# Attention in three scheduler streams, y stores on SyncE, issue times in the scheduler, and first gates during the last attention round

## The chip, the cores and the metric

The kernel runs on all 8 cores of one Trainium2 chip, one batch element of 4096 x 1024 tokens per core, with the same instructions on each. The metric is the device time of the slowest core in microseconds (us). Some executions of these kernels fall in a second, slower state, in which the four cores of one die show a lower TensorE clock (0.81 instead of 0.98 in the worst); only fast runs are compared here. Single cores of a fast run differ by some 30 us. Profiles are of the slowest core unless said.

## The reference, cut to what matters

One decoder layer. From the same input come the projections of 12 attention heads (three dilated causal windows) and of a state-space mixer; then per token

```python
z = h @ w_in                      # q | k | v | u | gates
y_attn = softmax-weighted sum over the three dilated windows
y_ssm  = glu(gelu(s5_ssm(u)))
mix = (sig(g1 + b) * (y_ssm @ w_ssm_proj) + sig(g2 + b) * (y_attn @ w_attn_proj)) @ w_out
h = LN(alpha * h + mix)
h = LN(alpha * h + relu(h @ w_up)**2 @ w_down)
```

The kernel does it in two stages. The mixed stage (the first 620 us) runs projections, attention in six rounds, and the state space of 32 groups side by side. The dense stage works off eight blocks of 512 tokens: GLU, gates, output projection, layer norm, and the large MLP. TensorE bounds it.

## The kernel before

The program notes every operation with a stream name and a priority, and a list scheduler then fixes the order of each engine's queue. Within a stream the order of an engine's operations is the program's; between streams the scheduler may choose. It has a cost for each operation and a rough model of the DMA queues.

```python
if op.dma:
    issue = 1000.0 if e == "pool" else 70.0     # ns that an issue takes of the engine
    free[e] = t + issue
    start = end = max(dma_free[e][0], t + issue)
    ...
```

State space, one of 32 groups: the result leaves PSUM through ScalarE, and ScalarE also issues its two stores.

```python
def ssm_y(g):
    ...
    cp("act", ysg.ap, bk.ap.rearrange("p (t c) -> p t c", t=2), [bk], [ysg])
    for t in range(2):
        dma("act", y_d[g, :, t * 8:t * 8 + 8].rearrange("h t c -> t h c"), ysg.ap[:, t, :], [ysg], [y_res.res[g * 2 + t]])
```

Attention is a single stream, "att". In the last rounds (g = 2) every bank is evicted and normalised:

```python
for (q, j) in units:
    qk(q, j)                 # scores, TensorE
    pt = ex(q, j)            # exp on ScalarE, times bias on VectorE
    if prev is not None:
        pv(*prev)            # products; after each 4th block: evac() and norm()
    prev = (q, j, pt)
```

Weights of the dense stage are float32 in memory. GpSimd's DMA queue casts most of them to bfloat16 scratch while attention runs, one cast after every third projection tile; w_up is cast in the first dense block itself.

```python
for name in ("glu", "gate", "sp", "ap", "out", "dn"):
    for i in range(len(wb[name][2].res) // 2):
        add_cast(name, i)

def pace(op, rnd, t):
    nonlocal evs
    evs += 1
    if rnd > 0 and evs % 3 == 0 and wcast:
        after = Res(); after.w = op
        wcast.pop(0)([after])
```

The softmax here doesn't subtract the row's maximum and nothing guards it: scores larger than these inputs give would overflow.

## Time and profile before

| | kernel before |
|---|---|
| median of fast runs | 2025.7 us (2023.1 to 2030.0) |
| TensorE busy | 1863.0 us, 92% |
| last scan of the state space | 571.0 us |
| last projection tile evicted | 546.7 us |
| first transposes of the dense stage | 688.4 us |
| TensorE's wait for w_up | 14.6 us |

The transposes of the first layer norm make a good clock: they come after exactly 271 matmuls of the dense stage, so their time says how far the work has come. The table by stretch, cut at such marks (columns: stretch, length, then busy us and instruction count of each engine, TensorE clock, DMA share, GB/s), for the kernel before:

```profile
core 3: us, PE busy (x) PEld busy (x) DVE busy (x) ACT busy (x) POOL busy (x), PEclk, DMA share, GB/s
200.00:546.70 346.70, 299.32 (x2737) 196.28 (x2737) 173.43 (x282) 163.43 (x245) 26.85 (x44) 0.95 0.76 149
546.70:688.40 141.70, 85.19 (x411) 38.86 (x412) 56.04 (x91) 46.70 (x65) 15.40 (x18) 0.74 0.60 180
688.40:827.60 139.20, 124.53 (x590) 56.59 (x589) 56.59 (x85) 50.11 (x71) 17.91 (x17) 0.95 0.91 215
```

The first line is the mixed stage to the last projection, the second the hole with the first 271 dense matmuls, the third the way to the transposes of block 1, which holds the wait for w_up. All engines but TensorE are at half load or less in the first two.

### The profile page before, as it was taken

Reading aid. Unit: us, or ns where it says so; the run is one execution under the profiler, and the core shown is the slowest. Engines: PE = TensorE matmul, PEld = TensorE weight load, DVE = VectorE, ACT = ScalarE, POOL = GpSimd, SP = SyncE. Lnnn points to the kernel's source line nnn. Section 1 sums busy time; section 2 is a strip of 40 time slices with the busy share of each in tenths; the row PEclk is TensorE's granted clock in tenths of the full one; section 3 lists DMA queues with packets and bytes.
Section 4 is the critical chain, followed back from the end, with each engine's and each line's share of the span. In section 5 each row is a group of like instructions: output and inputs, shape, how many; then the busy total and the mean of one; then the engine's idle time right before and its main releaser. Section 6 shows DMA issues by size and latency. Waiting matters only on the chain.

```text
span 2030.0 us, 30949 instructions; the slowest of 8 cores (2000.8 to 2030.0 us)
## 1 busy us (share of the span) xinstructions
PE 1863.0 (92%) x10468; PEld 927.2 (46%) x10468; DVE 947.2 (47%) x1444; ACT 669.9 (33%) x1037; POOL 171.0 (8%) x218
## 2 busy tenths in 40 slices
PE   4999799889737995999999999999999999999997
PEld 2554555555613442444444444444444444444443
DVE  5753355545642632553553364356345426535524
ACT  4555345545433531223214213322321322232120
POOL 2001000100001220000100200100010020010000
PEclk8999899989858997999999999999999999999998
DMA  9959888975475899364565547366355644743631
GB/s 168 200 170 186 165 155 163 161 135 114 130 215 189 201 195 273 130 238 146 172 224 198 157 164 258 125 225 236 135 171 201 225 140 167 249 141 135 228 120 42
DMA packets 133242, 357.62 MB, mean 176 GB/s; under 512 B 10720, under 2 KB 81248, under 8 KB 106848
## 3 DMA queue, kind: packets, MB, share of 16 engines
q1 hardware_dynamic: 73168, 256.96, 37.2%
q0 software_dynamic: 48336, 83.99, 23.2%
q10 hardware_dynamic: 11584, 14.68, 2.1%
q8 instruction: 88, 1.44, 0.3%
q14 instruction: 66, 0.54, 0.1%
HBM read 348.35 MB, written 72.88 MB: 207 GB/s over the span
## 4 chain that ended last, share of the span: by engine, by line
PE 83%; DMA 6%; ACT 3%; DVE 3%; issue 2%; ACTq 1%; another core or an unknown queue 1%; SPq 1%; POOL 0%; DVEq 0%; POOLq 0%
PE ps L481 82%; ACT arena L493 2%; DMA arena<-x_tile 1%; DMA arena<-sw_scratch 1%; ACTq L471 1%; DMA tab_scratch<-arena 1%; DMA ya_scratch<-arena 1%; DVE arena L511 1%; PE ps L486 1%; ACT arena L529 1%; DVE arena L522 1%; DMA y_scratch<-arena 1%; SPq L471 1%; DVE arena L530 0%
## 5 line engine op out<-in xcount | busy, mean ns | idle before, releaser
L481 PE MATMUL ps<-arena 128*128 128x512 bf16 (+4 forms) x10148 | 1853.2, 345 | 149.8 <-ACT arena L493 49.6
L481 PEld LDWEIGHTS ps<-arena 128*128 128x128 bf16 (+2 forms) x10148 | 909.7, 104 | 1074.9 <-issue 229.2
L493 ACT ACTIVATE arena<-ps 128x512 f32<-128x512 f32 (+2 forms) x384 | 260.5, 680 | 450.0 <-PE ps L481 351.3
L522 DVE SCALAR_TENSOR_TENSOR arena<-arena,ps 128x512 f32<-128x512 f32 (+1 forms) x288 | 191.2, 684 | 451.3 <-PE ps L481 416.7
L522 DVE SCALAR_TENSOR_TENSOR arena<-ps,arena 128x512 bf16<-128x512 f32 x256 | 176.8, 691 | 261.5 <-ACT arena L493 261.5
L511 DVE TENSOR_TENSOR arena<-arena 128x512 f32<-128x512 f32 (+6 forms) x291 | 170.1, 622 | 159.5 <-ACT arena L493 144.8
L522 DVE SCALAR_TENSOR_TENSOR arena<-arena 128x1024 f32<-128x1024 f32 (+2 forms) x163 | 189.0, 1159 | 64.5 <-ACT arena L493 38.7
L493 ACT ACTIVATE arena<-arena 128x512 f32<-128x512 f32 (+6 forms) x187 | 97.1, 525 | 273.1 <-DVE arena L1153 230.1
L529 ACT CAST arena<-ps 128x512 bf16<-128x512 f32 (+1 forms) x217 | 120.1, 570 | 155.4 <-PE ps L481 134.5
L493 ACT ACTIVATE arena<-ps,arena 128x512 f32<-128x512 f32 x128 | 87.7, 687 | 181.9 <-PE ps L481 181.9
L511 POOL TENSOR_TENSOR arena<-arena 128x512 bf16<-128x512 f32 x64 | 80.9, 1266 | 470.9 <-DVE arena L522 470.8
L1151 DVE BATCH_NORM_STATS2 arena<-arena 128x6 f32<-128x512 f32 x128 | 88.7, 693 | 10.7 <-DVE arena L522 0.2
L471 POOL DMA_DIRECT2D out<-arena x32 | 17.4, 545 | 693.5 <-DVE arena L522 686.1
L529 ACT COPY arena<-ps 128x512 f32<-128x512 f32 (+1 forms) x64 | 51.1, 799 | 67.3 <-PE ps L486 38.7
L493 ACT ACT_TABLE_LOAD x25 | 32.1, 1283 | 122.0 <-DVE arena L1153 105.5
L529 ACT CAST arena<-arena 128x1024 bf16<-128x1024 f32 x32 | 33.4, 1045 | 98.9 <-DVE arena L522 98.9
L511 DVE TENSOR_TENSOR arena<-arena,ps 128x512 f32<-128x512 f32 x64 | 41.1, 682 | 9.3 <-PE ps L481 9.3
L486 PE MATMUL ps<-arena 128*128 128x128 bf16 (+1 forms) x320 | 38.0, 236 | 2.8 <-DVE arena L511 2.8
L511 DVE TENSOR_TENSOR arena<-ps,arena 128x512 f32<-128x512 f32 (+1 forms) x33 | 22.7, 687 | 29.9 <-PE ps L481 18.4
L486 PEld LDWEIGHTS ps<-arena 128*128 128x128 bf16 (+1 forms) x320 | 30.1, 120 | 12.9 <-issue 4.7
L471 POOL DMA_DIRECT2D arena<-x x32 | 17.0, 532 | 113.2 <-DMA out<-arena 75.3
L831 DVE TENSOR_TENSOR_SCAN arena<-arena 128x256 f32<-128x256 f32 x32 | 22.2, 693 | 3.3
(26 smaller groups left out, 117.2 us busy)
## 6 DMA issues: line engine op xcount, KB each, us to landing
arena<-wb_dn SPq DMA_DIRECT2D x64, 1024.0 KB, 5.6
arena<-wb_up SPq DMA_DIRECT2D x56, 1024.0 KB, 9.4
arena<-wb_gate SPq DMA_DIRECT2D x32, 1024.0 KB, 10.3
arena<-wb_out SPq DMA_DIRECT2D x16, 1024.0 KB, 5.5
arena<-x POOLq DMA_DIRECT2D x32, 512.0 KB, 10.0
out<-arena POOLq DMA_DIRECT2D x32, 512.0 KB, 3.8
arena<-sw_scratch SPq DMA_DIRECT2D x32, 288.0 KB, 11.4
arena<-x_tile POOLq DMA_DIRECT2D x8, 1024.0 KB, 51.9
```

Of the source, the lines that this page charges most:

```text
L471: return P.add(eng, lambda e: e.dma_start(out=out, in_=in_), R(*reads), R(*writes), dma=True, pk=pk, svc=nb / run * pk / 16.0)
L481: return P.add("pe", lambda e: e.matmul(out, lhsT, rhs, start=start, stop=stop, **kw), R(*reads), R(*writes), cost=c)
L486: return P.add("pe", lambda e: e.transpose(out, in_, ident), R(*reads), R(*writes), cost=c)
L493: return P.add("act", lambda e: e.activation(out, in_, func, bias=bias, scale=scale), R(*reads), R(*writes), cost=c, aset=ASETS.get(func))
L511: return P.add(eng, lambda e: e.tensor_tensor(out, in0, in1, op), R(*reads), R(*writes), cost=ew_cost(eng, out, [in0, in1], True), lock=no ...
L522: return P.add("dve", lambda e: e.scalar_tensor_tensor(out, in0, scalar, in1, op0, op1), R(*reads), R(*writes), cost=160.0 + 1.06 * fsize( ...
L529: return P.add("act", lambda e: e.copy(out, in_), R(*reads), R(*writes), cost=c)
L831: P.add("dve", lambda e: e.tensor_tensor_scan(ws.ap, d0, t12.ap[:, 0, :], 0.0, ALU.mult, ALU.add), R(t12, rp), R(ws), cost=692.0, lock=True)
L1151: P.add("dve", (lambda hf_: lambda e: e.bn_stats(st6[:, hf_ * 6:hf_ * 6 + 6], xb.ap[:, hf_ * 512:hf_ * 512 + 512]))(hf), R(xb), R(m), cost ...
```

## The change

It means to let the engines overtake waits that stood in one queue, to take issue work off ScalarE, to give the scheduler true issue times, and to fill the last attention round with gates of the first dense block. The core of the diff, cuts marked with "...":

```diff
+    ISSUE = {"act": 600.0, "pool": 1000.0, "sp": 500.0}
...
-                issue = 1000.0 if e == "pool" else 70.0
+                issue = self.ISSUE[e]
...
+    def ssm_out(g):
+        ysg = ysb[g % 2]
+        cp("act", ysg.ap, banks[7].ap.rearrange("p (t c) -> p t c", t=2), [banks[7]], [ysg])
+        dma("sp", y_d[:, g].rearrange("q h t c -> q h (t c)"), ysg.ap.rearrange("p t c -> p (t c)"), [ysg], [y_res.res[g]])
...
-    PT = [ar.alloc([2, 512], BF16) for _ in range(2)]
+    PT = [ar.alloc([2, 512], BF16) for _ in range(3)]
-    yst = [ar.alloc([512], BF16) for _ in range(2)]
+    yst = [ar.alloc([512], BF16) for _ in range(3)]
...
-        for i in range(len(wb[name][2].res) // 2):
+        for i in range(4 if name == "dn" else len(wb[name][2].res) // 2):
...
-        if rnd > 0 and evs % 3 == 0 and wcast:
+        if rnd > 0 and evs % 4 == 0 and wcast:
...
         def evac(bank_no):
+            P.at("attv", 0)
...
         def norm(b):
+            P.at("norm", 1)
...
         def pv(q, j, pt):
+            P.at("attv", 0)
...
         for (q, j) in units:
+            P.at("att", 0)
...
+        if blk == 0:
+            brot = [6, 7]
+            for mq in range(2):
+                gp = load_piece("gate", mq, slot=None if mq else late)
+                for m in (2 * mq, 2 * mq + 1):
+                    held[m] = early[2 * m], early[2 * m + 1]
+                    gate(m, gp, 0, 0, held[m][0], AF.Identity)
+                    gate(m, gp, 256, 8, held[m][1], AF.Identity)
+                done(gp)
...
-        pcs2 = [load_piece("dn", 4 + q) for q in range(2)]
+        pcs2 = [load_piece("dn", 4 + q, blk == 0) for q in range(2)]
```

Smaller parts, cut: x tile 0 is loaded in four pieces; a block holds other rows of tokens (r and r + 8), so that one y store of 256 KB with 2 KB rows serves; three instead of five stores per batch of state-space weights; x rows and norm rows are loaded later; the bias factor is stored once and broadcast.

The diff also has a cast after every fourth projection tile, and four of the eight w_down pieces cast in block 0 instead of during attention.

More of the change, by code (lines that the diff above doesn't have):

```diff
@@ L394, in build_program @@
     xT_d = dram_in("x_tile", [8, 128, 8, 512])
-    xB_d = dram_in("x_blk", [8, 128, 8, 512])
+    xB_d = dram_in("x_blk", [8, 8, 128, 512])
     smP_d = dram_in("smalls_p", [128, SP_N])
@@ L413, in build_program @@
     u_d = dram_tmp("u_scratch", [4, 128, 16, 256], BF16)
-    y_d = dram_tmp("y_scratch", [32, 16, 16, 256], F32)
+    y_d = dram_tmp("y_scratch", [8, 32, 16, 2, 256], F32)
     ya_d = dram_tmp("ya_scratch", [2, 128, 16, 256], BF16)
@@ L423, in build_program @@
     u_res = Buf(None, 4)
-    y_res = Buf(None, 64)
+    y_res = Buf(None, 32)
     ya_res = Buf(None, 16)
     tabs_res = Buf(None, 16)
-    sw_res = Buf(None, 160)
+    sw_res = Buf(None, 96)
     mw_res = Buf(None, 4)
@@ L572, in build_program, with xres @@
     ar.seek(X0, Q0)
-    xT = ar.alloc([8, L], BF16, nres=8)
+    xT = ar.alloc([8, L], BF16, nres=11)
+    def xres(a, b):
+        return (xT.res[0:4] if a == 0 else []) + xT.res[3 + max(a, 1):3 + b]
     ar.seek(Q0, A0)
@@ L595, in build_program @@
     for item in ("u0", 0, "u1", "q0", "q1", 1, "q2", 2, 3, 4, 5, "u2", "u3", 6, 7, "s"):
-        if isinstance(item, int):
-            dma("pool", xT.ap[:, :, item * 512:(item + 1) * 512], xT_d[item], [], [xT.res[item]])
+        if item == 0:
+            for j in range(4):
+                dma("pool", xT.ap[:, 2 * j:2 * j + 2, 0:512], xT_d[0, :, 2 * j:2 * j + 2], [], [xT.res[j]])
+        elif isinstance(item, int):
+            dma("pool", xT.ap[:, :, item * 512:(item + 1) * 512], xT_d[item], [], xres(item, item + 1))
         elif item == "s":
@@ L613, in build_program @@
                     mm(bk.ap, wu[ft].ap[:, kc, :], xT.ap[:, kc, s * 512:(s + 1) * 512], kc == 0, kc == 7,
-                       [wu[ft], xT.res[s]], [bk])
+                       [wu[ft]] + (xres(s, s + 1) if s else [xT.res[kc // 2]]), [bk])
                 cp("act", ub.ap.rearrange("p (i f) c -> p f i c", f=2)[:, :, :, s * 32:(s + 1) * 32],
@@ L624, in build_program @@
     smB = ar.alloc([SB_N], F32)
-    dma("sp", smB.ap, smB_d, [xT.res[0]], [smB])
+    dma("sp", smB.ap, smB_d, [xT.res[3]], [smB])
     gcs = [ar.alloc([2, 3, 256], F32) for _ in range(2)]
@@ L737, in build_program @@
         cp("act", wx[:, :, :, 128:192], src[:, :, :, 0:64], [bk], [st.res[0]])
-        sres = [[sw_res.res[(g0 + j) * 5 + part] for j in range(GB)] for part in range(5)]
+        sres = [[sw_res.res[(g0 + j) * 3 + part] for j in range(GB)] for part in range(3)]
         dst = sw_d[g0:g0 + GB].rearrange("g p q -> p g q")
-        for k in range(2):
-            for hf in range(2):
-                dma("sp", dst[hf * 64:hf * 64 + 64, :, 384 + k * 256:640 + k * 256],
-                    st.ap[(hf ^ k) * 64:(hf ^ k) * 64 + 64, :, 384:640], [st.res[1]], sres[1 + 2 * k + hf])
-        dma("sp", dst[:, :, 0:384], st.ap[:, :, 0:384], [st.res[0]], sres[0])
+        for hf in range(2):
+            dma("sp", dst[hf * 64:hf * 64 + 64, :, 640:896], st.ap[(1 - hf) * 64:(1 - hf) * 64 + 64, :, 384:640],
+                [st.res[1]], sres[1 + hf])
+        dma("sp", dst[:, :, 0:640], st.ap, st.res, sres[0])
     ar.seek(argm.span[0], c1.span[0])
@@ L813, in ssm_in @@
             [u_res.res[ft]], [ug])
-        dma("sp", sw.ap, sw_d[g], sw_res.res[5 * g:5 * g + 5] + [mw_res.res[g // 8]], [sw])
+        dma("sp", sw.ap, sw_d[g], sw_res.res[3 * g:3 * g + 3] + [mw_res.res[g // 8]], [sw])
         for hf in range(2):
@@ L835, in ssm_y @@
     def ssm_y(g):
-        sw, ug, ysg = swb[g % NS], ugb[g % NS], ysb[g % 2]
+        sw, ug = swb[g % NS], ugb[g % NS]
         bk = banks[7]
@@ L845, in ssm_y @@
                 mm(y, sw.ap[:, o:o + 128], vv.ap[:, k, 0:256], False, k == 1, [sw, vv], [bk], skip_group_check=True)
-        cp("act", ysg.ap, bk.ap.rearrange("p (t c) -> p t c", t=2), [bk], [ysg])
-        for t in range(2):
-            dma("act", y_d[g, :, t * 8:t * 8 + 8].rearrange("h t c -> t h c"), ysg.ap[:, t, :], [ysg], [y_res.res[g * 2 + t]])
+    def ssm_out(g):
+        ysg = ysb[g % 2]
+        cp("act", ysg.ap, banks[7].ap.rearrange("p (t c) -> p t c", t=2), [banks[7]], [ysg])
+        dma("sp", y_d[:, g].rearrange("q h t c -> q h (t c)"), ysg.ap.rearrange("p t c -> p (t c)"), [ysg], [y_res.res[g]])
     for g in range(NS):
@@ L857, in build_program @@
             ssm_in(g + NS)
+        ssm_out(g)
         if g + 1 < 32:
@@ L863, in build_program @@
     ar.seek(S1)
-    PT = [ar.alloc([2, 512], BF16) for _ in range(2)]
-    eb = [ar.alloc([2, 512], BF16) for _ in range(2)]
+    PT = [ar.alloc([2, 512], BF16) for _ in range(3)]
+    eb = [ar.alloc([2, 256], BF16) for _ in range(2)]
     bst = [ar.alloc([2, 256], F32)]
     rn = ar.alloc([512], F32)
-    yst = [ar.alloc([512], BF16) for _ in range(2)]
+    yst = [ar.alloc([512], BF16) for _ in range(3)]
     def accres(h, rs, cs_):
@@ L911, in qk_tile @@
                 mm(bk.ap, w.ap[:, kc, :], xT.ap[:, kc, t * 512:(t + 1) * 512], kc == 0, kc == 7,
-                   [w, xT.res[t]], [bk])
+                   [w] + xres(t, t + 1), [bk])
             if g == 0:
@@ L937, in v_tile @@
                 xv = xT.ap[:, :, t0:t0 + 128 * dil].rearrange("p k (m q) -> p k q m", q=dil)[:, :, rho, :]
-                rd = xT.res[t0 // 512:(t0 + 128 * dil - 1) // 512 + 1]
+                rd = xres(t0 // 512, (t0 + 128 * dil - 1) // 512 + 1)
                 for kc in range(8):
@@ L966, in build_program @@
         dma("sp", bs.ap, biasT_d[rnd], [], [bs])
-        for k in range(2):
-            act(ebr.ap[:, :, k * 256:(k + 1) * 256], bs.ap, AF.Exp, [bs], [ebr])
+        act(ebr.ap, bs.ap, AF.Exp, [bs], [ebr])
         nseq = (1, 4, 16)[g]
@@ L992, in ex @@
             nonlocal pti
-            pt = PT[pti % 2]
+            pt = PT[pti % len(PT)]
             pti += 1
@@ L997, in ex @@
             act(pt.ap[:, :, 0:wid], s, AF.Exp, [banks[2], banks[3]], [pt], scale=0.125)
-            tt("dve", pt.ap[:, :, 0:wid], pt.ap[:, :, 0:wid], ebr.ap[:, :, 0:wid], ALU.mult, [pt, ebr], [pt])
+            if wid == 512:
+                p4 = pt.ap.rearrange("p h (b c) -> p h b c", b=2)
+                tt("dve", p4, p4, ebr.ap[:, :, None, :].to_broadcast([128, 2, 2, 256]), ALU.mult, [pt, ebr], [pt])
+            else:
+                for c0, c1_ in ((0, 256), (256, 384)):
+                    tt("dve", pt.ap[:, :, c0:c1_], pt.ap[:, :, c0:c1_], ebr.ap[:, :, 0:c1_ - c0], ALU.mult, [pt, ebr], [pt])
             return pt
         def evac(bank_no):
+            P.at("attv", 0)
             for h in range(2):
@@ L1025, in norm @@
             nonlocal ysi
-            ys_ = yst[ysi % 2]
+            P.at("norm", 1)
+            ys_ = yst[ysi % len(yst)]
             ysi += 1
@@ L1053, in pv @@
                         norm(b // 4)
+                        P.at("attv", 0)
                 if has_next and not full:
@@ L1072, in build_program @@
     ar.seek(E0, S1)
-    ring = [ar.alloc([4096], BF16)]
+    late = ar.alloc([4096], BF16)
+    xTb = ar.alloc([8, 512], BF16)
     yf = ar.alloc([4, 512], F32, nres=4)
-    xTb = ar.alloc([8, 512], BF16)
     yT = ar.alloc([4, 512], BF16)
     ar.seek(X0, Q0)
-    ring += [ar.alloc([4096], BF16) for _ in range(7)]
+    ring = [ar.alloc([4096], BF16) for _ in range(7)] + [late]
     mixin = ar.alloc([8, 512], BF16, nres=8)
@@ L1083, in build_program @@
     sgs = [ar.alloc([512], F32) for _ in range(3)]
-    lnr = [ar.alloc([D], F32) for _ in range(4)]
+    lnr0 = ar.off
+    early = [ar.alloc([512], F32) for _ in range(8)]
+    earlies = ar.t[:, early[0].span[0] // 4:early[7].span[1] // 4]
+    ar.seek(lnr0, Q1)
     ar.seek(Q1, A0)
@@ L1096, in build_program @@
     sgs.append(ar.alloc([512], F32))
-    P.at("p3w", 6)
-    for i in range(4):
-        dma("pool", lnr[i].ap, lnrows_d[i], [], [lnr[i]])
     live = set()
+    fresh = {id(r): i for i, r in enumerate(ring)}
     bi = 0
@@ L1121, in last_use, with load_piece @@
     def last_use(slot):
+        if id(slot) in fresh:
+            return fresh[id(slot)]
         rs = slot.res[0]
         return max([o.seq for o in list(rs.r.values()) + rs.rd] + [rs.w.seq if rs.w is not None else 0])
-    def load_piece(name, i, first=False):
-        slot = min((r for r in ring if id(r) not in live), key=last_use)
+    def load_piece(name, i, first=False, slot=None):
+        slot = slot or min((r for r in ring if id(r) not in live), key=last_use)
         live.add(id(slot))
+        fresh.pop(id(slot), None)
         dst, src, res, sz = wb[name]
@@ L1161, in build_program, with load_xb @@
     outr = out_d.rearrange("(c r) d -> r c d", r=16)
-    rows = lambda d, blk, t: d[2 * blk + t // 2, (t % 2) * 128:(t % 2) * 128 + 128, :]
+    rows = lambda d, blk, t: d[blk + 8 * (t // 2), (t % 2) * 128:(t % 2) * 128 + 128, :]
     xslot = lambda blk, t: xs[(blk % 2) * 4 + t]
+    def load_xb(blk):
+        P.at("p3l", 6)
+        dma("pool", xTb.ap, xB_d[blk].rearrange("k p c -> p k c"), [], [xTb])
     def load_g(blk):
         P.at("p3l", 6)
-        dma("pool", xTb.ap, xB_d[blk], [], [xTb])
@@ L1168, in load_g @@
         for kc in range(4):
-            src = y_d[kc * 8:(kc + 1) * 8].rearrange("g h t c -> (g h) t c")[:, 2 * blk:2 * blk + 2, :]
-            dma("sp", yf.ap[:, kc, :].rearrange("p (t c) -> p t c", t=2), src,
-                [y_res.res[(kc * 8 + j) * 2 + blk // 4] for j in range(8)], [yf.res[kc]])
+            dma("sp", yf.ap[:, kc, :], y_d[blk, kc * 8:(kc + 1) * 8].rearrange("g h t c -> (g h) (t c)"),
+                y_res.res[kc * 8:kc * 8 + 8], [yf.res[kc]])
         act(yT.ap, yf.ap, AF.Gelu_apprx_tanh, [yf], [yT])
@@ L1173, in load_g, with gate @@
         for p4 in range(2):
-            dma("sp", yab.ap[:, p4, :].rearrange("p (r c) -> p r c", r=2), ya_d[p4, :, 2 * blk:2 * blk + 2, :],
-                [ya_res.res[p4 * 8 + blk]], [yab.res[p4]])
-    def stage_g(blk):
+            dma("sp", yab.ap[:, p4, :].rearrange("p (r c) -> p r c", r=2), ya_d[p4, :, blk::8, :],
+                [ya_res.res[p4 * 8 + blk // 2], ya_res.res[p4 * 8 + 4 + blk // 2]], [yab.res[p4]])
+    def gate(m, piece, off, col, sg, func=AF.Tanh):
+        bk = nbk()
+        for kc in range(8):
+            mm(bk.ap, pv3(piece)[:, kc, off + m % 2 * 128:off + (m % 2 + 1) * 128], xTb.ap[:, kc, :], kc == 0, kc == 7,
+               [piece, xTb], [bk])
+        act(sg.ap, bk.ap, func, [bk, bgate], [sg], bias=bgate.ap[:, col + m:col + m + 1], scale=0.5)
@@ new lines, in stage_g @@
+    def stage_g(blk):
+        nonlocal brot
+        load_xb(blk)
+        P.at("p3", 7)
+        held = {}
+        if blk == 0:
[7 more added lines that the diff above has]
+                done(gp)
+            brot = [0, 1, 6, 7]
@@ L1191, in stage_g @@
         done(wg_)
-        gp = [load_piece("gate", 0)]
+        if held:
+            for j in range(2):
+                e_ = early[4 * j:4 * j + 4]
+                o_ = earlies[:, j * 2048:j * 2048 + 2048]
+                act(o_, o_, AF.Tanh, e_, e_)
+        gp = {} if held else {0: load_piece("gate", 0)}
         wsp_, wap_ = load_piece("sp", 0), load_piece("ap", 0)
@@ L1197, in stage_g @@
             mq, m2 = m // 2, m % 2
-            if m2 == 0 and mq < 3:
-                gp.append(load_piece("gate", mq + 1))
-            pv = pv3(gp[mq])
-            b_gs, b_ga, b_ps, b_pa = nbk(), nbk(), nbk(), nbk()
-            for off, bk in ((0, b_gs), (256, b_ga)):
-                for kc in range(8):
-                    mm(bk.ap, pv[:, kc, off + m2 * 128:off + (m2 + 1) * 128], xTb.ap[:, kc, :], kc == 0, kc == 7,
-                       [gp[mq], xTb], [bk])
+            if m2 == 0 and 2 * mq + 2 < 8 and 2 * mq + 2 not in held:
+                gp[mq + 1] = load_piece("gate", mq + 1)
+            if m in held:
+                gsb, gab = held[m]
+            else:
+                gsb, gab = nsg(), nsg()
+                gate(m, gp[mq], 0, 0, gsb)
+                gate(m, gp[mq], 256, 8, gab)
+            b_ps, b_pa = nbk(), nbk()
             for kc in range(4):
@@ L1211, in stage_g @@
                    [wap_, yab], [b_pa])
-            gsb, gab = nsg(), nsg()
-            act(gsb.ap, b_gs.ap, AF.Tanh, [b_gs, bgate], [gsb], bias=bgate.ap[:, m:m + 1], scale=0.5)
-            act(gab.ap, b_ga.ap, AF.Tanh, [b_ga, bgate], [gab], bias=bgate.ap[:, 8 + m:9 + m], scale=0.5)
             stt(gsb.ap, gsb.ap, 1.0, b_ps.ap, ALU.add, ALU.mult, [b_ps, gsb], [gsb])
@@ L1217, in stage_g, with load_x @@
             tt("pool", mixin.ap[:, m, :], gsb.ap, gab.ap, ALU.add, [gsb, gab], [mixin.res[m]])
-            if m2 == 1:
+            if m2 == 1 and m not in held:
                 done(gp[mq])
         done(wsp_, wap_)
-    def load_x(blk):
+    def load_x(blk, after=()):
         P.at("p3x", 6)
@@ L1225, in load_x @@
             x_ = xslot(blk, t)
-            dma("pool", x_.ap, rows(xr, blk, t), [], [x_])
+            dma("pool", x_.ap, rows(xr, blk, t), after, [x_])
     def stage_o(blk, t, wo):
@@ L1280, in stage_d @@
             dma("pool", rows(outr, blk, t), x_.ap, [x_], [])
-    load_x(0)
     stage_g(0)
+    load_x(0, [mixin.res[0]])
+    P.at("p3w", 6)
+    ar.seek(lnr0, Q1)
+    lnr = [ar.alloc([D], F32) for _ in range(4)]
+    for i in range(4):
+        dma("pool", lnr[i].ap, lnrows_d[i], [], [lnr[i]])
+    P.at("p3", 7)
     wo = [load_piece("out", oh) for oh in range(2)]
@@ L1288, in build_program @@
     done(*wo)
-    load_x(1)
     stage_g(1)
+    load_x(1, [mixin.res[0]])
     for blk in range(NB):
@@ L1310, in build_program @@
             done(*wo)
-        pcs2 += [load_piece("dn", 6 + q) for q in range(2)]
+        pcs2 += [load_piece("dn", 6 + q, blk == 0) for q in range(2)]
         for t in range(TB):
@@ L1374, in make_in_maps @@
                          x_tile=c_(x.reshape(8, 512, 8, 128).transpose(0, 3, 2, 1)),
-                         x_blk=c_(x.reshape(256, 8, 2, 8, 128).transpose(1, 4, 3, 2, 0).reshape(8, 128, 8, 512))))
+                         x_blk=c_(x.reshape(256, 2, 8, 8, 128).transpose(2, 3, 4, 1, 0).reshape(8, 8, 128, 512))))
     return maps
```

## The prediction

> **What bounds the kernel now.** First the spans of the cores: 2000.8 to 2030.0 us, both dies at clock 0.96, so no core is special. Then the page's slices of the slowest core, 50.75 us each.
>
> ```profile
> PE   4999799889737995999999999999999999999997
> PEclk8999899989858997999999999999999999999998
> DMA  9959888975475899364565547366355644743631
> ```
>
> TensorE (PE) is busy 92% of the span, and from slice 16 on it is full. What can be won lies left of that: slice 0 (the first x tiles), the mixed stage of slices 4 to 10 (projections, attention, state space), the hole in slices 11 and 12, and slice 15. A table by stretch gives the sizes:
>
> ```profile
> core 3: us, PE busy (x) PEld busy (x) DVE busy (x) ACT busy (x) POOL busy (x), PEclk, DMA share, GB/s
> 200.00:546.00 346.00, 299.32 (x2737) 196.28 (x2737) 172.83 (x281) 162.73 (x244) 26.85 (x44) 0.95 0.76 149
> 546.00:626.00 80.00, 23.92 (x139) 11.98 (x139) 34.44 (x57) 29.77 (x41) 4.72 (x9) 0.56 0.69 206
> 626.00:777.00 151.00, 149.80 (x704) 67.81 (x704) 63.60 (x95) 59.83 (x83) 28.58 (x26) 0.98 0.82 194
> 777.00:791.00 14.00, 0.45 (x2) 0.14 (x2) 0.69 (x1) 0.60 (x1) 0.00 (x0) 0.65 1.04 220
> 791.00:2030.00 1239.00, 1223.54 (x5824) 560.38 (x5822) 570.70 (x832) 311.29 (x486) 93.73 (x109) 0.99 0.50 178
> ```
>
> The last projection leaves TensorE at about 546 us, the first GLU matmul of the dense stage starts at 626.12. In those 80 us TensorE does 139 small matmuls, at half clock: the largest loss, 56 us. Nobody is busy there (VectorE 34, ScalarE 30 of 80 us), so it is latency of one chain. The waits of TensorE from 555 to 660, and the timeline of one turn, name it:
>
> ```profile
> PE ps L481 <- ACT arena L493: 39.7, 6, 14.1
> PE ps L481 <- DVE arena L511: 11.3, 15, 4.7
> ```
>
> ```profile
> 592.61 2.07 ACT L493 ACTIVATE arena<-arena 64x512 f32<-64x512 f32 x3 [1.41 <-DVE arena L511]
> ...
> 604.94 1.48 DVE L522 SCALAR_TENSOR_TENSOR arena<-arena 64x512 bf16<-64x512 f32 x2 [11.88 <-DMA ya_scratch<-arena]
> ...
> 606.92 0.81 ACT L493 ACTIVATE arena<-ps 128x768 bf16<-128x768 f32 x1 [12.24 <-DVE arena L522]
> ...
> 607.88 0.51 PE L481 MATMUL ps<-arena 64*128 64x256 bf16 x4 [14.09 <-ACT arena L493]
> ```
>
> Read upwards: scores wait for the next exponential, which stands behind the store of the normalised output, which waits for VectorE, which waits for one of two staging buffers that a store is still reading (that store took 24.8 us, among eight weight pieces asked for at 573 to 578). Even undisturbed, a bank (two exponentials, two multiplies, eviction, Ln/Ln/Exp, two products) took 8.2 us here: normalisations start at 576.25, 584.55 and 592.61.
>
> **What the Trainium skill says.** "TensorE: Matmul & The Clock Gate", Part 1: an array idle for a window of about 3.4 us falls to half clock and needs as long to return. The trace agrees: clock 0.56 in the hole; the first dense matmuls after it start 0.43 us apart, later ones 0.216 (695 in 150.00 us). "PSUM — Partial Sum Buffer", Engine vs sequencer instructions: ScalarE and VectorE queues are strict FIFO. The lines above are that. "DMA: Bandwidth & Descriptors", Issuing engines are not separate DMA queues: all engines' DMAs share 16 DMA engines, issuing elsewhere saves sequencer time alone. The trace has the price: an issue of a y store holds ScalarE's queue 0.607 us (median), 64 times. "ScalarE: Activation LUTs", What ACT_TABLE_LOAD costs: 1283 ns a load; the page's 25 loads average 1283.
>
> **The change, part by part.** I compared the instruction orders of the two built kernels.
>
> *Three streams.* Scores, products and normalisation may now overtake each other; three probability and three staging buffers instead of two. In the old order 100 attention and 39 state-space matmuls come after the last projection matmul (the 139 of the table). In the new one the state space ends 369 projection matmuls before that point, 72 attention matmuls follow it, and gates and GLU stand between them.
>
> *First gates early.* Gates of the first four of eight column tiles in block 0: 4 x 2 x 8 = 64 matmuls. With the first GLU matmuls, 76 dense-stage matmuls lie before the last attention matmul, 17 of them before the last projection. 76 x 0.216 = 16.4 us leave the dense stage. Cost: 8 extra evictions (0.69 us each) and two wide Tanh (1.9 us) on ScalarE, some table loads: about 13 us, on an engine idle half the time.
>
> *The hole, summed.* Work that moves ahead of the last projection: 39 state-space matmuls (0.11 us warm, 4.3), 28 attention ones (0.1, 2.8), 17 gates (3.7): 10.8 us of TensorE. Then four banks of attention remain. ScalarE needs per bank 2 x 0.81 + 2.07 + 0.33 (store issue) + about 1.0 (gate evictions) = 5.0 us; VectorE 2 x 0.75 + 1.28 + 1.48 = 4.3. Four banks: 20, with drain 24 us. The dense stage's zero point is then 546 + 10.8 + 24 - 16.4 = 564 where it was 626: **-62 us**. Both output halves that block 0 needs are banks 0 and 4, so the last normalisations hold nothing up.
>
> *y stores on SyncE*, one of 256 KB with 2 KB rows instead of two with 1 KB: 64 x 0.607 = 39 us of ScalarE queue gone, and its waits for these stores (10.7 us in 200 to 546). SyncE takes 32 issues; with 5 instead of 6 or so DMAs of 0.5 to 0.6 us a group it stays far under one group's 10 us. TensorE was idle 47 us in 200 to 546, a third of it behind ScalarE. I take **-10 us** for this, the better order there and the warmer clock.
>
> *First x tile in four parts.* The first matmul waited until 15.2 us, may now start earlier, but 48 matmuls later the second tile (34.7 us) holds all, and that is the DMA's rate: **0**, three extra issues at most +1.
>
> *Loads moved.* x rows, norm rows and x of block 1 come during the first dense blocks, not before. TensorE waited 14.6 us for the w_up pieces at 777; DMA was saturated from 671 (share 1.0). In 620 to 800 the casting queue moved 12.57 MB at 45% of the engines, 6.4 us a MB, the plain one 24.1 MB at 38.9%, 2.9 us a MB. Some 2 MB to 3 MB more plain loads in that stretch: **+8 us** on the w_up wait. Four w_down pieces are cast in block 0 instead of during attention: 4 x (6.4 + 2.9) against 4 x 2.9, 26 us more DMA time, against some 32 us free in the 50 us after 812 (share 0.36): mostly hidden, **+4 us**.
>
> Sum: -62 - 10 + 8 + 4 = -60, less rounding and issue +1: 2027 - 59 = **1968 us**. All later blocks are TensorE at its rate and keep their 171 us.
>
> **Rivals.** (1) *The hole only moves.* The state space now has to run about 45% faster relative to the projections; if its loads (11 us to land) or the chain through VectorE can't follow, TensorE waits in 250 to 480 and loses there what the hole gave. For it: 16.2 us of VectorE waiting for table loads, y stores that took 16 to 26 us. Against: VectorE and ScalarE are at half load there and loads run four groups ahead. Half of the gain back: 2000 us. (2) *DMA becomes the bound at the start of the dense stage.* The stage starts 60 us earlier, with 4 MB more to load and 4 pieces more to cast; w_up and w_down waits could grow to 30 to 45 us: 1985 to 1995. For it: share 1.04 while TensorE stood still. Against: in 626 to 671 the share was 0.35, and most loads are paced by TensorE's own progress. (3) *The mixed stage gains more*: if the stretch 200 to 546 packs as tightly as 101 to 203 (idle 3.2 of 50.7 a slice instead of 6.5), another 20 us and its cold clock: 1940. (4) *A wide broadcast multiply on VectorE loses its fast form*: at most 54 x 0.5 = 27 us, spread on an engine half idle: a few us.
>
> **Range and chances.** Centre 1968; the mixed stage is uncertain by 20 either way, DMA by +20/-10, the hole by 12. Eight in ten: 1940 to 2000. The 2% line is 1986.4, 18 us above the centre: faster 0.78, within 2% 0.20, slower 0.02 (it would need a new wait of 100 us).
>
> **What would show it.** Right: from the last projection to the first run of dense matmuls some 25 us instead of 80, with gate matmuls in it; clock there near 1; no TensorE wait over 5 us behind ScalarE or an output store; ScalarE queue without y stores; a w_up wait of 15 to 25 us; each later block still 171 us; first stretch to 34 us unchanged. Wrong: TensorE idle in 200 to 546 well over 47 us (rival 1), or over 30 us idle for w_up, w_down or x in the first dense block (rival 2). A total under 1940 would mean that I under-counted the mixed stage.

## The result and the profile after

The changed kernel takes 1954.5 us (median of 4 fast runs, 1950.6 to 1956.6) against 2025.7. The ratio is 0.9644, 95% interval 0.9619 to 0.9669. Ratios here are those of one kernel's fast runs against the other's in the same rounds, so not quite the ratio of the medians. Where a ratio is turned into us below, it is times 2027.

The slices of the page after (48.9 us each) answer to those in the prediction:

```profile
PE   5899999899989868999999999999999999999997
PEclk8999999899999989999999999999999999999998
DMA  9968787787479997645563764556376445635531
```

The hole (a 3 and a 7 in slices 11 and 12, counted from 0) is gone; an 8, a 6 and an 8 in slices 13 to 15 are the largest loss left after slice 0, and DMA stands at 9 in the first two of them. The table by stretch, cut at the same marks as before (to 0.3 us):

```profile
core 3: us, PE busy (x) PEld busy (x) DVE busy (x) ACT busy (x) POOL busy (x), PEclk, DMA share, GB/s
200.00:513.50 313.50, 295.82 (x2777) 198.48 (x2775) 184.83 (x329) 168.28 (x251) 21.81 (x35) 0.97 0.72 154
513.50:591.00 77.50, 66.22 (x322) 28.79 (x321) 43.47 (x74) 43.72 (x56) 15.55 (x17) 0.93 0.85 268
591.00:743.50 152.50, 129.20 (x592) 57.74 (x591) 56.94 (x85) 50.08 (x71) 22.19 (x23) 0.92 1.00 226
```

Compare line with line. The mixed stage is 33 us shorter though it holds more matmuls: TensorE is busy 94% of it, not 86%. The stretch with the hole and the first dense matmuls (271 before, 17 fewer now, as these come before the last projection) is 64 us shorter, at clock 0.93 instead of 0.74. The way to block 1 is 13 us longer. The five largest waits of TensorE over the whole run (total, times, longest), before and then after:

```profile
PE ps L481 <- ACT arena L493: 53.4, 19, 14.1
PE ps L481 <- DMA arena<-x_tile: 25.2, 2, 15.2
PE ps L481 <- DVE arena L511: 23.8, 24, 4.9
PE ps L481 <- DMA arena<-w_up: 14.6, 2, 13.6
PE ps L481 <- ACT arena L529: 12.2, 10, 4.1
```

```profile
PE ps L482 <- DMA arena<-x_tile: 23.4, 5, 11.0
PE ps L482 <- DMA arena<-w_up: 23.2, 3, 13.0
PE ps L482 <- ACT arena L530: 18.4, 7, 6.8
PE ps L482 <- DMA arena<-w_down: 6.9, 1, 6.9
PE ps L482 <- DVE arena L523: 6.3, 2, 5.0
```

L493, L511 and L529 are L494, L512 and L530 after. Before, 53.4 us of waiting stood behind ScalarE's exponentials and other activations (L493) and 23.8 behind VectorE's L511; now these are 3.1 and 1.9 us. What is left is DMA, at the start and for w_up and w_down, and ScalarE's copies out of PSUM (L530), 18.4 us instead of 12.2. After the w_down wait nothing differs: the long run of 695 matmuls that recurs in each block takes 150.00 us in both kernels.

The end of attention in the changed kernel, ScalarE's timeline (start, us, what):

```profile
538.66 1.28 ACT L494 ACT_TABLE_LOAD   x1
539.96 0.60 ACT L494 ACTIVATE arena<-ps 128x512 f32<-128x512 f32 x1
540.42 0.33 ACTq L472 DMA_DIRECT2D ya_scratch<-arena  x1
540.85 0.60 ACT L494 ACTIVATE arena<-ps 128x512 f32<-128x512 f32 x1 [0.30 <-issue]
541.47 1.28 ACT L494 ACT_TABLE_LOAD   x1
542.76 2.07 ACT L494 ACTIVATE arena<-arena 64x512 f32<-64x512 f32 x3
545.09 1.28 ACT L494 ACT_TABLE_LOAD   x1 [0.26 <-PE ps L482]
```

The GLU's Tanh (L494, 128x512 from PSUM) and the last banks' Ln and Exp (64x512) alternate, and each turn costs a table load: 31 loads in all instead of 25. They sit in a stretch where ScalarE has room.

### The profile page after: what moved, and what is told of

It reads as the page before. It is cut to its first block, busy times and chain, and to the rows that moved or that the text cites. A ratio compares the mean times of both kernels' runs of the same rounds, so it can differ in the third digit from the quotient of the medians.

```text
span 1955.0 us, 30811 instructions; the slowest of 8 cores (1923.8 to 1955.0 us)
## 1 busy us (share of the span) xinstructions
PE 1850.7 (95%) x10468; PEld 923.0 (47%) x10468; DVE 953.7 (49%) x1486; ACT 675.7 (35%) x1039; POOL 174.7 (9%) x217
## 4 chain that ended last, share of the span: by engine, by line
PE 85%; DMA 9%; ACT 2%; issue 1%; SPq 1%; another core or an unknown queue 1%; DVE 1%; POOL 0%; ACTq 0%; DVEq 0%; POOLq 0%
PE ps L482 84%; DMA y_scratch<-arena 3%; DMA arena<-w_up 2%; DMA arena<-x_tile 1%; DMA arena<-w_down 1%; DMA tab_scratch<-arena 1%; ACT arena L494 1%; SPq L472 1%; PE ps L487 1%; DVE arena L523 0%; POOL arena L472 0%; ACT L494 0%; ACT arena L530 0%; DVE arena L512 0%
## 5 line engine op out<-in xcount | busy, mean ns | idle before, releaser
L494 ACT ACTIVATE arena<-ps 128x512 f32<-128x512 f32 (+2 forms) x384 | 260.6, 680 | 410.4 <-PE ps L482 343.9
L512 DVE TENSOR_TENSOR arena<-arena 128x512 f32<-128x512 f32 (+7 forms) x333 | 176.6, 563 | 101.4 <-ACT arena L494 88.5
L494 ACT ACTIVATE arena<-arena 128x1 f32<-128x1 f32 (+9 forms) x183 | 97.2, 537 | 267.2 <-DVE arena L1176 239.8
L530 ACT CAST arena<-ps 128x512 bf16<-128x512 f32 (+1 forms) x217 | 120.5, 571 | 132.8 <-PE ps L482 115.9
L494 ACT ACTIVATE arena<-ps,arena 128x512 f32<-128x512 f32 x128 | 87.7, 687 | 172.2 <-PE ps L482 171.0
L512 POOL TENSOR_TENSOR arena<-arena 128x512 bf16<-128x512 f32 x64 | 81.0, 1267 | 528.7 <-DVE arena L523 451.4
L494 ACT ACT_TABLE_LOAD x31 | 39.8, 1283 | 123.5 <-DVE arena L1176 106.5
L530 ACT COPY arena<-ps 128x512 f32<-128x512 f32 (+1 forms) x64 | 51.1, 799 | 64.0 <-PE ps L487 36.8
L530 ACT CAST arena<-arena 128x1024 bf16<-128x1024 f32 x32 | 33.5, 1045 | 97.7 <-DVE arena L523 97.7
L512 DVE TENSOR_TENSOR arena<-arena,ps 128x512 f32<-128x512 f32 x64 | 41.4, 682 | 15.8 <-PE ps L482 15.5
L512 DVE TENSOR_TENSOR arena<-ps,arena 128x512 f32<-128x512 f32 (+1 forms) x33 | 22.8, 690 | 25.3 <-PE ps L482 25.1
L531 DVE COPY arena<-ps 128x512 f32<-128x512 f32 x32 | 20.7, 685 | 12.5 <-PE ps L482 12.2
L534 DVE RECIPROCAL arena<-arena 128x1 f32<-128x1 f32 (+1 forms) x65 | 10.7, 164 | 28.5 <-ACT arena L494 28.0
```

What stands on the lines that cost most here:

```text
L494: return P.add("act", lambda e: e.activation(out, in_, func, bias=bias, scale=scale), R(*reads), R(*writes), cost=c, aset=ASETS.get(func))
L512: return P.add(eng, lambda e: e.tensor_tensor(out, in0, in1, op), R(*reads), R(*writes), cost=ew_cost(eng, out, [in0, in1], True), lock=no ...
L530: return P.add("act", lambda e: e.copy(out, in_), R(*reads), R(*writes), cost=c)
L531: return P.add(eng, lambda e: e.tensor_copy(out, in_), R(*reads), R(*writes), cost=c, lock=not in_psum(in_))
L534: return P.add("dve", lambda e: e.reciprocal(out, in_), R(*reads), R(*writes), cost=160.0 + 6.2 * fsize(out))
```

## The experiments

Twelve kernels, each timed over three rounds, all correct. The last four (casts and streams together, and the three with w_up pieces) ran on another chip than the first eight, so they are compared by ratio. Five marks for each, from the profile of the slowest core; "dense mark" is the first transposes, after 271 dense matmuls (279 in the one-stream kernel). "Order" is how many of the 2304 projection matmuls stand ahead of the last state-space matmul in the built order of TensorE's queue.

| kernel | order | last scan | last projection | dense mark | block 1 mark | ratio |
|---|---|---|---|---|---|---|
| before | 2304 | 571.0 | 546.7 | 688.4 | 827.6 | 1 |
| before + streams | 2304 | 571.8 | 548.1 | 685.1 | 826.3 | 0.9974 |
| before + casts | 1936 | 460.0 | 522.7 | 640.6 | 780.5 | 0.9841 |
| before + casts + streams | 1875 | 451.9 | 518.2 | 609.3 | 753.0 | 0.9701 |
| changed | 1932 | 453.3 | 513.2 | 591.3 | 743.5 | 0.9644 |
| changed, one stream | 1936 | 449.7 | 509.3 | 619.2 | 772.4 | 0.9824 |
| changed, cast every third tile | 2304 | 497.4 | 500.0 | 610.7 | 772.5 | 0.9746 |
| changed, no early gates | 1932 | 449.6 | 514.5 | 602.3 | 755.3 | 0.9709 |
| changed, y stores on ScalarE | 1586 | 405.7 | 507.8 | 582.8 | 736.7 | 0.9609 |
| changed, old issue times | 1935 | 439.4 | 504.2 | 580.9 | 734.6 | 0.9614 |
| changed, nudged | 1932 | 444.0 | 510.0 | 584.8 | 739.6 | 0.9644 |
| changed, four w_up pieces cast during attention | 1935 | 472.0 | 536.5 | 615.5 | 742.2 | 0.9655 |
| the same, y stores on ScalarE | 1606 | 451.1 | 548.3 | 626.1 | 750.3 | 0.9695 |
| the same, old issue times too | 1541 | 427.7 | 549.3 | 629.1 | 752.5 | 0.9708 |

The first theory was that the streams had closed both the hole and the idle time of the mixed stage. Its rivals: ScalarE freed of y store issues, and the order made with true issue times. The first four runs undo one part each.

**One stream.** The three P.at lines put back:

```diff
-            P.at("attv", 0)
+            P.at("att", 0)
-            P.at("norm", 1)
+            P.at("att", 0)
```

> The changed kernel with scores, products and normalisation put back into one stream (all else kept: buffers, early gates, y stores on SyncE, issue times). My theory: the streams are what closed both the hole after the last projection and the idle time of the mixed stage; without them 1995 to 2015 us, TensorE idle in the mixed stage back to over 35 us and the last projection some 25 us later than 514 us. Rival, that ScalarE freed of y store issues did it: 1960 to 1975 us, mixed stage idle under 25 us.

1987.7 us, ratio 0.9824 (0.9787 to 0.986): 36 us lost, half of the change. But not where expected. The last projection is as early as ever (509 us), and the stretch to the dense mark is what grew, from 77.5 to 109.9 us. Its table by stretch:

```profile
200.00:509.30 309.30, 290.37 (x2696) 191.13 (x2695) 179.05 (x309) 160.69 (x238) 20.61 (x33) 0.96 0.75 155
509.30:619.20 109.90, 80.09 (x406) 34.94 (x405) 57.07 (x102) 58.26 (x74) 16.31 (x18) 0.83 0.67 206
```

TensorE is busy 94% of the mixed stage without the streams too. So the streams close the hole, and something else shortened the mixed stage. The theory fell in that half.

**y stores on ScalarE.**

```diff
-        dma("sp", y_d[:, g]...
+        dma("act", y_d[:, g]...
```

> The changed kernel with the 32 y stores issued by ScalarE again (same size and layout, 256 KB each). My theory (streams did it): 1953 to 1963 us. Rival (ScalarE's queue time did it): 32 x 0.6 = 19 us of queue back plus waits behind it, 1975 to 1990 us, last projection 20 us later.

1947.3 us, 0.9609 (0.958 to 0.9639): nothing lost; if anything some 7 us gained (the two intervals overlap). The rival of ScalarE's queue time is refuted. In the changed kernel ScalarE waits for earlier y stores 18.3 us (200 to 560), more than the 10.7 us before, so the waits behind these stores did not leave with the issues. They are most of what TensorE still loses in the mixed stage: ScalarE's copies at 228.6, 287.0 and 372.1 us had waited 5.5, 2.7 and 9.0 us for an earlier y store (there are two buffers to store from), and each time TensorE went on 0.7 us later, after 4.7, 1.9 and 6.8 us of idling. That is 13.4 of its 17.7 idle us there. More buffers were not tried.

**Old issue times.**

```diff
-    ISSUE = {"act": 600.0, "pool": 1000.0, "sp": 500.0}
+    ISSUE = {"act": 70.0, "pool": 1000.0, "sp": 70.0}
```

> The changed kernel whose scheduler takes 70 ns for a DMA issue of ScalarE and SyncE again, as the kernel before did (order alone changes). My theory: within 8 us of 1954. Rival, that the mixed stage gained from an order made with true issue times: 1970 to 1990 us and TensorE idle in 200 to 500 us up from 16 to over 35 us.

1947.0 us, 0.9614 (0.9597 to 0.9631). The true issue times bring nothing here either, and this rival falls too.

**No early gates.**

```diff
-        if blk == 0:
+        if False:
```

> The changed kernel without early gates: all eight column tiles' gates of block 0 are computed in the dense stage. My theory: 64 x 0.216 = 13.8 us of TensorE return to the dense stage, and a little cold clock, 1966 to 1972 us. Rival, that the start of the dense stage is bound by the casting loads and gives early work back as a longer w_up wait: 1954 to 1960 us, with the w_up wait down from 23 to about 10 to 15 us.

1968.6 us, 0.9709 (0.9677 to 0.9741): 13 us lost, as 64 x 0.216 = 13.8 says. The w_up wait is 25.6 us, no shorter than the 23.2 with early gates. An earlier start of the dense stage is not given back there: the slowest core of the kernels with the changed loads needs 152 to 155 us from the dense mark to block 1's, early or late. There are two exceptions, below: casts every third tile (161.8 us, on a core with a lower clock) and the kernels with w_up pieces.

Streams and gates made 49 of 72 us, and the early end of the state space was still without a cause. Comparing built orders of variants, without running them, showed it: of all parts of the changed kernel, the digit in the cast pacing decides whether the state space ends in the middle of the last rounds or at their end. That was the second theory, tested with the next four.

**Cast every third tile.** One digit:

```diff
-        if rnd > 0 and evs % 4 == 0 and wcast:
+        if rnd > 0 and evs % 3 == 0 and wcast:
```

> The changed kernel with one digit put back: a weight cast is let go after every third projection tile instead of every fourth (the number of casts stays 26). Theory C (cast pacing): the scheduler, which models the cast queue, then sees the state-space loads come late and orders the state space to the end (built order: last state-space matmul with all 2304 projection matmuls done, instead of 1932). The hole comes back: last scan after 500 us, no gates before the last projection, 1980 to 2000 us. Rival S (streams, buffers and merged y stores did the rest): within 10 us of 1954.

1977.6 us, 0.9746 (0.9712 to 0.9781): 21 us lost, and the last scan moves to 497 us. The expected 500 and 1980 were missed narrowly, the direction not. But TensorE's mixed stage is fuller than with the digit at 4, and the last projection comes even earlier. State space and last round are left over for the end, and 110.7 us pass to the dense mark:

```profile
200.00:500.00 300.00, 290.44 (x2752) 195.25 (x2750) 182.93 (x326) 161.16 (x243) 18.96 (x31) 0.98 0.74 149
500.00:610.70 110.70, 73.08 (x346) 31.69 (x344) 44.24 (x79) 43.76 (x58) 16.35 (x18) 0.81 0.80 221
```

The profiled run is the slowest of the five (1993.7 us; clock 0.96 on cores 4 and 5, 0.97 to 0.98 on the others). Core 3, at 0.97, has nearly the same marks: last projection at 501.5, dense mark 108.8 us later. So the digit opens the hole again, and is not what filled the mixed stage of the changed kernel. With the state space late no gate may start early, because gates use its two PSUM banks.

**Casts alone, in the kernel before.**

```diff
-        for i in range(len(wb[name][2].res) // 2):
+        for i in range(4 if name == "dn" else len(wb[name][2].res) // 2):
-        if rnd > 0 and evs % 3 == 0 and wcast:
+        if rnd > 0 and evs % 4 == 0 and wcast:
-        pcs2 = [load_piece("dn", 4 + q) for q in range(2)]
+        pcs2 = [load_piece("dn", 4 + q, blk == 0) for q in range(2)]
```

(and the same for the last two w_down pieces)

> The kernel before with the cast changes alone: every fourth tile, four w_down pieces cast in block 0 instead of during attention. Theory C: the state space ends some 80 to 120 us earlier (before 490 us instead of 571), the last projection 25 to 40 us earlier, 1980 to 1995 us in spite of 8 to 10 us more w_down wait. Rival S: 2020 to 2035 us.

1999.6 us, 0.9841 (0.9805 to 0.9877): 32 us gained with no other part of the change. The last scan comes 111 us earlier, the last projection 24 us. The median is 5 us above the range expected. These are two edits in one, the digit and four w_down pieces fewer during attention; no run has one of them alone in the kernel before.

**Streams alone, in the kernel before.** The P.at lines of the diff and nothing else, two buffers kept.

> The kernel before with the three streams alone. Undone in the changed kernel they cost 33 us. Theory C: in the old order the state space still ends last, so the streams only shorten the turns of the hole: 2005 to 2015 us. Rival S (the streams are worth the same wherever they are): 1990 to 1997 us.

2027.0 us, 0.9974 (0.9928 to 1.002): no difference is shown, less than either theory expected. (The profiled core ran part of its first 200 us at a lower clock; another core of this run has its dense mark 2 us earlier than the same core of the kernel before.) The same lines that are worth 36 us in the changed kernel are worth 5 here, 15 at the end of the interval. The trace shows what holds the hole open. Attention's matmuls now end at 574.9 us, not at 617.4, but then TensorE waits for ScalarE's GELU of the state space's output, and the last that this waited for were the loads of y, issued at 580 to 592 us, behind the last y stores:

```profile
623.15 48.82 PE L481 MATMUL ps<-arena 128*128 128x512 bf16 x215 [48.29 <-ACT arena L493]
619.80 1.28 ACT L493 ACT_TABLE_LOAD   x1 [8.10 <-DMA arena<-y_scratch]
```

So two chains run through the hole, attention's and the state space's, and with one shortened the other still ends near 620 us.

**A nudge without meaning.** The scheduler's slack for ScalarE, 215 ns instead of 200:

```diff
-    SLACK = {"pe": 600.0, "act": 200.0, ...
+    SLACK = {"pe": 600.0, "act": 215.0, ...
```

> The changed kernel with one number of the scheduler nudged that means nothing (slack of ScalarE 215 ns instead of 200). How far does an order differ in time for no reason? If within 3 us of 1954, then the 7 us that y stores on ScalarE and old issue times gained are those edits' own; if 5 to 10 us off, these are the list scheduler's scatter.

Ratio 0.9644 (0.9593 to 0.9694), that of the changed kernel, from the two fast runs of six (1954.1 and 1960.6 us). Four runs (2190 to 2268 us, the cores of one die at clock 0.81 to 0.87) are left out. This nudge shows no scatter, but its interval is 10 us wide to either side, and one nudge can't say that there is none.

**Casts and streams together, in the kernel before.** The two edits above.

> The kernel before with the cast changes and the three streams, and nothing else. Alone they gave 31 and 3 us. Theory (each needs the other: casts move the state space forward, streams then let the last round run without standing behind normalisation): together 55 to 62 us, 1966 to 1975 us, close to the changed kernel without early gates (1969). Rival (they add up): 1988 to 1996 us.

1970.2 us, 0.9701 (0.9683 to 0.972): 61 us, where the two alone gave 32 and 5. The streams need the casts: they are worth 5 us without them and 28 with them. Its stretch from the last projection to the dense mark:

```profile
518.20:609.30 91.10, 72.64 (x336) 31.84 (x341) 41.05 (x66) 46.62 (x59) 14.84 (x17) 0.87 0.72 233
```

91 us against 118 with casts alone and 142 before. And 0.9701 is the time of the changed kernel without early gates (0.9709). So casts, streams and early gates make up the whole gain; once the first two are there, y stores on SyncE, merged stores, issue times, split x tile, third buffers and later loads sum to nothing, within the 7 us or so that these intervals leave. What they do without the casts' digit was not taken apart: the changed kernel with the digit put back is still 51 us faster than the kernel before, where streams alone gave 5.

The last three aimed at what was left, the wait for w_up.

**Four w_up pieces cast during attention.**

```diff
-    for name in ("glu", "gate", "sp", "ap", "out", "dn"):
-        for i in range(4 if name == "dn" else len(wb[name][2].res) // 2):
+    for name, i0, i1 in (..., ("out", 0, 2), ("up", 4, 8), ("dn", 0, 4)):
+        for i in range(i0, i1):
-            piece = load_piece("up", up, blk == 0)
+            piece = load_piece("up", up, blk == 0 and up < 4)
```

> The changed kernel with four of the eight w_up pieces cast during attention too, so block 0 casts half as many. Theory: the w_up wait of 23 us comes from the casting queue in the first dense block; it falls below 8 us and the half clock after it goes too: 1930 to 1942 us. Rival: the wait is plain DMA bandwidth, or the eight extra casts slow attention by as much: 1950 to 1960 us.

1960.2 us, 0.9655 (0.9638 to 0.9673): no gain over the changed kernel. The wait itself went as the theory says; waits of TensorE from 600 to 900:

```profile
PE ps L482 <- DMA arena<-w_down: 10.5, 1, 10.5
PE ps L482 <- DMA arena<-w_up: 2.9, 1, 2.9
```

From the dense mark to block 1's it takes 126.7 us instead of 152.5, the second exception named above. But the dense mark itself comes at 615.5 us, 24 us later. GpSimd's timeline at the start of the run shows why:

```profile
1.62 2.82 POOL L472 DMA_DIRECT2D wb_dn<-w_down  x4 [0.92 <-POOLq L384]
4.25 0.77 POOL L472 DMA_DIRECT2D arena<-w_u  x1
4.79 3.03 POOL L472 DMA_DIRECT2D arena<-x_tile  x4
```

The 34 casts are four more than the 30 turns that the pacing has. The four left over are issued with nothing to wait for, and the scheduler put them first of all, ahead of the first weights and x tile. TensorE's first matmul went from 11.0 to 33.8 us, and the second x tile from 34.1 to 55.1: 21 us lost at the start. This is a fault of the experiment, not of the idea. The attention stage did not suffer from eight more casts: TensorE was busy 331.3 of the 336.5 us from 200 to its last projection. A kernel that also paces these four has not been run. Estimated from these two measurements, 1960 - 21, it would take some 1940 us.

**The same, with y stores on ScalarE.** The edits of the two kernels.

> As c8_up4, with the y stores issued by ScalarE again. If the 7 us that this gained on the changed kernel are its own, 1924 to 1935 us and 7 us under c8_up4; if they were the scheduler's scatter, within 3 us of c8_up4.

1966.2 us, 0.9695 (0.9678 to 0.9713): 8 us slower than the one above, where y stores on ScalarE had gained 7 before. So the gain of 7 us, if it is one, is no property of the edit that could be carried over; it depends on the order around it.

**And with old issue times too.**

> As c10_up4_ya, and with the old issue times in the scheduler too. In the built order the state space ends earliest of all (1541 of 2304 projection matmuls done). If ending it earlier still pays: 3 to 8 us under c10_up4_ya. If it is off the end's path once it is ahead of the last round: the same within 3 us.

1973.8 us, 0.9708 (0.9687 to 0.973): not faster than the one above. Its last scan is at 427.7 us, its last projection at 549.3. Ending the state space still earlier does not pay by itself.

No version that beats the changed kernel by more than the 7 us of the second and third run was found; those two, at 0.9609 and 0.9614, are the fastest measured.

## Why the prediction was right or wrong

The time, 1954.5, lies in the range of 1940 to 2000, 14 us under the centre, and clearly faster was the likeliest outcome. Going through the sum with the marks of the slowest core (a gain of 75 us there):

- **The hole, -62: near in size, the mechanism half right.** By the term's own sum, the stretch from the last projection to the dense mark was to shrink by 72 us (24 instead of 80 us, and 16.4 of dense work done early); it shrank by 64. Undoing streams or gates opens it by 32 and 10 us, and the waits behind ScalarE that the prediction read are gone. But it counted the state space's move out of the hole under "Three streams", and streams alone leave the state space last and the stretch at 137 us. And "564 where it was 626" had the last projection 10.8 us later, which is where the sum misses.
- **The mixed stage, "I take -10 us": the mis-sized term.** With the 10.8 us of added work the last projection was to come about 1 us later; it came 33 us earlier. This is the step that failed: "for this, the better order there and the warmer clock", "this" being y stores off ScalarE. The runs show no gain from y stores or issue times. In the kernel before, the cast pacing with fewer casts alone brings the last projection 24 us earlier, and TensorE's idle time from 200 us to there from 47 to about 30; with the streams it is about 26, in the changed kernel 18. The prediction saw that the state space ends earlier in the new order and put it down to the streams; it read the casts only as DMA time. But the digit is not the cause of the fuller stage by itself: with it put back, the changed kernel idles only 10 us there. Whether the four fewer casts fill it, or another part does, stays open. A small misreading stands beside it: of the 47 us idle, 19.5 stood behind ScalarE (12.5 behind L493, 7.0 behind L529), two fifths and not a third. Rival 3 (a gain in this stage of 20 us more) was the one that came.
- **w_up, +8: right for the wait, too small for the stage.** The wait grew by 8.6 us (14.6 to 23.2), and restarts below full clock come on top (32 matmuls in 8.9 and 9.8 us, where 0.216 us each make 6.9; before there was one, of 9.1): 13.3 us from mark to mark. The mechanism, casting loads on a full DMA, is supported by the run that halved them.
- **w_down, +4: too small.** A wait of 6.9 us, and 9.2 us longer from block 1's mark to block 2's (180.3 against 171.1). Only four of the eight cores pay it (179.5 to 181.6 us); the others take 171.0 to 171.6.
- **x tile in four, 0: right.** First matmul 11.0 instead of 15.2 us, second tile 34.1 instead of 34.7.
- **Rival 1 (the hole only moves)** did not come about: TensorE idles 18 us of the mixed stage after 200 us, not 47. **Rival 2 (DMA the bound at the start of the dense stage)** came in part: 30.1 us of waiting for w_up and w_down. Its reason, that an earlier start is given back, is not seen in the run without early gates, which starts 11 us later. **Rival 4** (a slow broadcast multiply) was not tested by itself; VectorE is busy 953.7 us in all against 947.2.

That the total is only 14 us off is in part luck. On the slowest core the mixed stage gave 34 us more than the sum had, the hole 8 less, and w_up and w_down cost 10 more; the errors partly cancel.

What is open, besides the fuller mixed stage: why the pacing of casts moves the state space so far in the scheduler's order. The likeliest reading is that its DMA model lets casts push the state-space loads back, but no run takes the model apart. That it is the order and not the DMA load on the chip is supported by the kernel with eight more casts, whose mixed stage stayed full (5 us idle).

## What to carry to other kernels

When a list scheduler makes the order, look up which numbers feed its model, however far they seem from the engine that bounds: in the changed kernel a pacing digit for background loads decided where a whole stage of the work ended (last scan at 453 or 497 us). Compare the built orders of variants first, which costs nothing, and then test the parts both alone and by undoing, since two parts that gave 32 and 5 us gave 61 together. When a wait is removed, look which chain ends next: here the state space's stood right behind attention's. And this scheduler placed four transfers without a dependency first of all; background transfers need an explicit release.

## What the Trainium skill lacked or had wrong

- "TensorE: Matmul & The Clock Gate", Part 1: on the default power profile (which one this chip has is not on record) it advises to budget 13/16 of the clock for dense matmuls on all cores. In the profiled run of the changed kernel all eight cores show clock 1.00 from 1000 to 1900 us, with TensorE busy 895 us of the 900 or more; 695 matmuls take 150.00 us, 0.216 us each. A clock near 13/16 (0.8125) does occur: in two slow runs of the nudged kernel, die 1 stood at 0.808 to 0.815 on average. It is a state of some runs here, not of all.
- "ScalarE: Activation LUTs", What ACT_TABLE_LOAD costs: 1283 ns for the load is right, but the further drain of 1380 ns is not seen here. In the lines above an activation ends at 541.45, a load starts at 541.47 and lasts 1.28 us, and the next activation starts at 542.76 us.
- "DMA: Bandwidth & Descriptors", SWDGE vs HWDGE vs iDMA, gives no price of a cast in a DMA, nor does another page. Here, from 620 to 800 us of the kernel before, the GpSimd queue (mostly casts) held 45.0% of the engines for 12.57 MB and the plain queue 38.9% for 24.10 MB: 6.4 against 2.9 us of all engines a MB. But these MB are those written: a w_up piece counts 1024 KB, its bfloat16 size, and twice that is read. With ten such casts in the stretch (10.5 MB), some 23 MB were read, 3.5 us a MB (an estimate from these sizes). The packets differ too, 1.4 KB on average against 4.7, and no run separates the two.
